# Feed-forward products by seven: two of the four weight sums per block as accumulating transfers, their products one step later, and an eighth raw weight tile

## The chip, the core and the metric

The kernel runs on one core of one Trainium2 chip. The metric is the device time of one execution in microseconds (us), as the median of several runs. TensorE (PE) multiplies, with its weight loads shown apart as PEld; VectorE is DVE, ScalarE is ACT, GpSimd is POOL, and SyncE is SP, which here only issues transfers. [...]

## What is computed

Two decoder layers on 256 tokens of width 2048, all in float32. Each layer has a mixing part (a gated spatial unit beside windowed attention) and a feed-forward part. The change touches the feed-forward part and, by the same function, the product for the attention queries.

```python
for l in range(DEPTH):                       # DEPTH = 2
    h = rms_norm(x, norm1_g[l])
    z = h @ w_in[l]                          # u, v, q, k, v columns
    ...                                      # spatial gating and attention
    x = x + mixed @ w_out[l]
    h2 = rms_norm(x, norm2_g[l])             # 256 x 2048
    x = x + (jax.nn.silu(h2 @ w_gate[l]) * (h2 @ w_up[l])) @ w_down[l]   # D_FF = 5632
```

## The kernel before, in words

**Products in three matmuls.** A float32 weight tile of 128x1024 (512 KB) is loaded into a tile called `raw` by SP (line 103, `raw_load`). `split2` splits it in two float32r parts: ACT casts it to `wh` (line 112), and DVE subtracts, `wl = raw - wh` (line 113). Each product of 128 columns is then three matmuls of 128x512 (lines 146 to 148): wh with the high part of the activations, wl with the high part, wh with the low part. There are seven raw tiles, five wh and four wl. A load on SP waits until a raw tile comes free, which is when the last DVE instruction that reads it is done; loads stand in one order on SP's queue.

**Units.** A standard unit (`unit`, line 150) is one raw tile and 12 matmuls into two PSUM banks (`dacc` or `acc`): the down projection, one gate-and-up block of the eleven, the input and output projections. A half unit (`s_unit` inside `seven`, line 300) is one raw tile and 6 matmuls into one bank `m0` to `m4`.

**Seven products instead of eight.** `seven` (line 297) treats gate and up (the two column halves) and even and odd rows of the weights as a 2x2 matrix, and computes it with seven half-size products. It has four steps, i = 0 to 3, and then eight half units. A step loads three raw tiles: `b11` (gate, even), `b12` (up, even) and `b22` (up, odd), and makes three sums of 128x1024:

- `b11 += b12` on DVE (line 328), for product m1;
- `t2 = b11 + b22` on DVE (line 329), for product m3;
- `b12 += b22` for product m2. On DVE it is line 335. In the query product of the first layer alone (`s_by_dma`) it is line 331 instead: POOL issues a transfer that reads b22's weights from memory again and adds them into b12.

After m3's split POOL issues a second accumulating transfer, which adds the fourth weight (gate, odd) into t2 (line 337); t2 is kept for the eight half units at the end. The half units of a step stand in the order m0, m1, m3, m4, m2 (in a call with `soon`, m4 comes second in its first step).

**The order of the work.** Ten of eleven gate-and-up blocks go through `seven` in each layer (20 blocks in all), 30 half units each. Between them standard units of the down projection are dealt out in a fixed share (83 units to 300 half units, about 1.4 per step). The program is written in this order; a scheduler then sets the order on each engine from the dependencies and its own costs, so the built order is what the excerpts below show. The query products are dealt out between the units of the input projection by the same means (`q_to`).

**Others on POOL's queue.** In the first layer POOL's queue also holds the power of the RMS norms (`ir`, line 202), the load of the gating weights `wm` (line 596, after the first `ir`) and an `AFFINE_SELECT` on them (line 597), which zeroes the upper triangle.

Of the kernel before, what the change touches and what calls it, by code (L numbers as in the profile page):

```python
# [12 lines left out]
F32 = mybir.dt.float32  # L13
# [7 lines left out]
P = 128  # L21
# [13 lines left out]
NB = 512  # L35
# [6 lines left out]
S_BLOCKS = (1, 2, 3, 4, 5, 6, 7, 8, 9, 10)  # L42
# [39 lines left out]
def trunk(ctx, tc, x, xt, w_in, w_q, w_out, w_gate, w_up, w_down, sgu_w, sgu_g, consts,  # L82
# [4 lines left out]
    wp = ctx.enter_context(tc.tile_pool(name="wp", bufs=1))  # L87
# [9 lines left out]
        return t.bitcast(F32)  # L97

    def raw_load(src, parts=1):
        raw = wp.tile([P, 2, NB], F32, tag="raw", name="raw", bufs=7)  # L100
        n = 2 // parts
        for i in range(parts):
            nc.sync.dma_start(raw[:, i * n : (i + 1) * n, :], src[:, i * n : (i + 1) * n, :])
        return raw

    def split2(raw):
        wh = wp.tile([P, 2, NB], F32R, tag="wh", name="wh", bufs=5)
        wl = wp.tile([P, 2, NB], F32R, tag="wl", name="wl", bufs=4)
        step = 2 if clock[0] > 1 else 1
        for j in range(0, 2, step):  # L110
            src = raw[:, j : j + step, :]
            nc.scalar.copy(wh[:, j : j + step, :], src)  # L112
            nc.vector.tensor_tensor(  # L113
                wl[:, j : j + step, :], src, f(wh[:, j : j + step, :]), ALU.subtract
            )
        return wh, wl
# [5 lines left out]
    def later(delay, fn):  # L122
        pending.append((clock[0] + delay, next(serial), fn))

    def tick(w=1.0):
        clock[0] += w
        due = sorted((e for e in pending if e[0] <= clock[0]), key=lambda e: e[:2])
        pending[:] = [e for e in pending if e[0] > clock[0]]
        for e in due:
            e[2]()  # L130
# [14 lines left out]
    def mm3(acc, ah, al, wh, wl, first, last, again=False):  # L145
        nc.tensor.matmul(acc, ah, wh, start=first, stop=False, skip_group_check=again)  # L146
        nc.tensor.matmul(acc, ah, wl, start=False, stop=False, skip_group_check=again)  # L147
        nc.tensor.matmul(acc, al, wh, start=False, stop=last, skip_group_check=again)  # L148

    def unit(src, acts, acc, first, last, again=False):  # L150
        raw = raw_load(src, 2 if clock[0] < 4 else 1)
        wh, wl = split2(raw)
        for j in range(2):
            act, aj = acts[j]
            for t in range(NTOK):
                ts = slice(t * P, (t + 1) * P)
                mm3(
                    acc[t], act[:, 0, aj, ts], act[:, 1, aj, ts], wh[:, j, :], wl[:, j, :],
                    first and j == 0, last and j == 1, again,
                )  # L160
        tick()
# [132 lines left out]
        extend(g, ap, "big", ext)  # L294
        return pair

    def seven(src, pairs, ext, out, end=lambda sg: None, soon=False, s_by_dma=False):
        bank = [pa.tile([P, NB], F32, tag="acc", name=f"m{i}") for i in range(5)]

        def s_unit(raw, m, i, op, first, last):  # L300
            wh, wl = split2(raw)
            for j in range(2):
                ah, al = (op(2 * i + j, h) for h in range(2))
                mm3(
                    bank[m], ah, al, wh[:, j, :], wl[:, j, :], first and j == 0,
                    last and j == 1, m in (0, 2),
                )
            tick(0.5)

        def a_op(k, t):  # L310
            return lambda p, h: pairs[p][:, h, k, t * P : (t + 1) * P]

        def e_op(n):
            return lambda p, h: ext[p][:, h, n, :]

        kept = []
        for i in range(4):
            b11 = raw_load(src(0, 0, i))
            b12 = raw_load(src(0, 1, i))
            b22 = raw_load(src(1, 1, i))  # L320
            t2 = ap.tile([P, 2, NB], F32, tag="spt", name="t2", bufs=4)
            first, last = i == 0, i == 3
            s_unit(b11, 0, i, a_op(0, 0), first, last)
            yield
            if soon and first:
                s_unit(b22, 4, i, e_op(3), first, last)
                yield
            nc.vector.tensor_tensor(b11, b11, b12, ALU.add)  # L328
            nc.vector.tensor_tensor(t2, b11, b22, ALU.add)
            if s_by_dma:  # L330
                nc.gpsimd.dma_start(b12, src(1, 1, i), accum_op=ALU.add)
            s_unit(b11, 1, i, e_op(1), first, last)
            yield
            if not s_by_dma:
                nc.vector.tensor_tensor(b12, b12, b22, ALU.add)
            s_unit(t2, 3, i, e_op(2), first, last)
            nc.gpsimd.dma_start(t2, src(1, 0, i), accum_op=ALU.add)  # L337
            yield
            if not (soon and first):
                s_unit(b22, 4, i, e_op(3), first, last)  # L340
                yield
            s_unit(b12, 2, i, e_op(0), first, last)
            yield
            kept.append(t2)
        m0, c12, c21, c22 = (
            zp.tile([P, NB], F32, tag="z", name=v) for v in ("m0", "c12", "c21", "c22")
        )
        nc.scalar.copy(m0, bank[0])
        nc.vector.tensor_tensor(m0, bank[3], m0, ALU.add)
        yield  # L350

        def add(out, x, y):
            nc.vector.tensor_tensor(out, x, y, ALU.add)

        steps = {
            0: lambda: add(c21, bank[2], m0),
            1: lambda: (nc.scalar.copy(bank[2], c21), add(c12, bank[1], m0)),
            2: lambda: (add(c22, bank[1], c21), add(c12, bank[4], c12)),
            5: lambda: out(0, bank[0], m0, c12),
        }  # L360
        for i in range(8):
            if i < 4:
                s_unit(raw_load(src(1, 0, i)), 0, i, a_op(1, 0), False, i == 3)
            else:
                s_unit(kept[i - 4], 2, i - 4, a_op(1, 1), False, i == 7)
            yield
            steps.get(i, lambda: None)()
        later(1, lambda: out(1, bank[2], c21, c22))
        end([m0, c21])
        yield  # L370

    def q_product(lay, pairs, ext):
        q = {"k": 0}
        q["steps"] = seven(
            lambda r, c, i: w_q[lay, c, i, r], pairs, ext, lambda *a: q["out"](*a),
            soon=True, s_by_dma=lay == 0,
        )
        return q

# [29 lines left out]
    for i in range(2 * NTOK):  # L409
        later(7 + 2.5 * i, lambda i=i: load_x(i // 2, i % 2))  # L410
    now_q = q_product(0, pairs1, ext1)

    for lay in range(L):
# [370 lines left out]
        def release(live=live, held=held, act_T=act_T):  # L784
            while held and live[0] < ACT_TILES:
                live[0] += 1
                act_T(*held.pop(0))

        def act_later(b, sg, held=held, release=release):
            for c in range(2):  # L790
                def ready(c=c):
                    held.append((b, c, sg))
                    release()

                later(2 + c, ready)
# [5 lines left out]
        def s_block(b, lay=lay, pairs2=pairs2, ext2=ext2, gated=gated, act_later=act_later):  # L801
            return seven(
                lambda r, c, i: (w_gate, w_up)[c][lay, b, i, r], pairs2, ext2, gated,
                lambda sg: act_later(b, sg), soon=b == S_BLOCKS[0],
            )

        seven_done = [False]
# [1 line left out]
        def s_stream(s_block=s_block):  # L809
            for b in S_BLOCKS:  # L810
                yield from s_block(b)
# [123 lines left out]
        if lay < L - 1:  # L935
            now_q = q_product(lay + 1, pairs1, ext1)
# [97 lines left out]
```

## Time and profile before

| | us |
|---|---|
| median of 3 runs | 1926.99 (1926.62 to 1929.71) |
| the profiled execution's own time | 1928.89 |
| its span in the trace | 1927.1 |
| PE busy | 1914.2 (99%), clock 1.0 |
| DVE busy | 1734.8 (90%) |
| ACT busy | 1341.1 (70%) |
| POOL busy | 150.5 (8%) |
| transfers, mean rate | 225 GB/s, 432.71 MB |

The busy share of PE says only that some matmul was in flight: a matmul of 128x512 takes about 390 ns and the next one starts 227 ns later, so PE can lose some 160 ns at a start before an idle stretch shows. What PE waits for is therefore read from PEld, whose loads carry the waits. The feed-forward parts run from about 300 to 930 us and from about 1256 to 1890 us of the span; in them the row of tenths for DVE stands at 9 throughout.

### The profile page before, as it was taken

What the parts mean: (1) busy time and instruction counts of PE and PEld (TensorE: products, weight loads), DVE (VectorE), ACT (ScalarE), POOL (GpSimd) and SP (SyncE); (2) the same over time, 40 slices, a digit from 0 to 9 for tenths busy, and PEclk for the clock granted to TensorE, in tenths of its full rate; (3) what the DMA queues carried; (4) which work ended last, traced back from release to release, by engine and by line L of the source; (5) the groups of instructions that cost most, each with busy time, mean ns of one, the idle gap of its engine ahead of it and who ended that gap; (6) DMA issues with size and microseconds to landing.
All of it is one profiled execution on the core that took longest, in us unless ns stands there. A gap on an engine that the chain in (4) does not pass through costs nothing.

```text
span 1927.1 us, 25136 instructions
## 1 busy us (share of the span) xinstructions
PE 1914.2 (99%) x8788; PEld 1568.1 (81%) x8788; DVE 1734.8 (90%) x1866; ACT 1341.1 (70%) x1799; POOL 150.5 (8%) x132
## 2 busy tenths in 40 slices
PE   9999999999999999999999999999999999999999
PEld 7788888877888888888888888888878888888887
DVE  7986689999999999999896767799999999999993
ACT  8768577677677676777777576666777677666674
POOL 0511000000000000000011200000000000000000
PEclk9999999999999999999999999999999999999999
DMA  9964347768777787778567534576778777867773
GB/s 337 283 255 155 136 159 219 239 217 274 210 239 242 248 258 222 224 237 277 190 216 260 184 128 165 176 244 208 236 246 257 225 225 245 274 207 242 240 260 122
DMA packets 120943, 432.71 MB, mean 225 GB/s; under 512 B 13424, under 2 KB 14064, under 8 KB 120816
## 3 DMA queue, kind: packets, MB, share of 16 engines
q1 hardware_dynamic: 105264, 375.52, 52.9%
q0 software_dynamic: 14976, 54.53, 15.5%
q8 instruction: 69, 1.13, 0.2%
q10 hardware_dynamic: 576, 1.05, 0.2%
q14 instruction: 58, 0.48, 0.1%
HBM read 428.95 MB, written 2.10 MB: 224 GB/s over the span
## 4 chain that ended last, share of the span: by engine, by line
PE 91%; DVE 3%; ACT 2%; issue 2%; DMA 1%; SPq 0%; POOL 0%; ACTq 0%; DVEq 0%; POOLq 0%
PE m L147 13%; PE m L148 13%; PE m L146 13%; PE dacc L146 10%; PE dacc L147 10%; PE dacc L148 10%; PE acc L146 6%; PE acc L147 5%; PE acc L148 5%; DVE wl L113 2%; ACT wh L112 1%; PE ps_v L568 1%; PE ps_f L219 1%; DMA raw<-in_w_in_dram 1%; PE ps_s L519 1%
## 5 line engine op out<-in xcount | busy, mean ns | idle before, releaser
L112 ACT CAST wh<-raw 128x1024 fp32r<-128x1024 f32 (+1 forms) x794 | 812.5, 1049 | 413.6 <-DVE raw L328 202.7
L113 DVE TENSOR_TENSOR wl<-raw,wh 128x1024 fp32r<-128x1024 f32 (+1 forms) x794 | 945.9, 1219 | 85.0 <-PE acc L147 28.5
L146 PE MATMUL m<-wh,ext 128*128 128x512 f32 x704 | 277.3, 395 | 1.6 <-ACT wh L112 1.6
L147 PE MATMUL m<-wl,ext 128*128 128x512 f32 x704 | 277.5, 394 | 1.4 <-DVE wl L113 1.4
L148 PE MATMUL m<-wh,ext 128*128 128x512 f32 x704 | 274.8, 390 | 0.0
L147 PE MATMUL dacc<-wl,aT 128*128 128x512 f32 x624 | 243.7, 391 | 0.3
L146 PE MATMUL dacc<-wh,aT 128*128 128x512 f32 x624 | 242.1, 392 | 1.8 <-ACT wh L112 1.8
L148 PE MATMUL dacc<-wh,aT 128*128 128x512 f32 x624 | 243.2, 390 | 0.0
L113 DVE TENSOR_TENSOR wl<-t,wh 128x1024 fp32r<-128x1024 f32 x176 | 212.3, 1220 | 5.6 <-PE dacc L147 3.0
L112 ACT CAST wh<-t 128x1024 fp32r<-128x1024 f32 x176 | 184.3, 1051 | 31.6 <-PE m L148 11.7
L146 PE MATMUL m<-wh,hT 128*128 128x512 f32 x528 | 205.6, 389 | 0.0
L148 PE MATMUL m<-wh,hT 128*128 128x512 f32 x528 | 205.4, 389 | 0.0
L147 PE MATMUL m<-wl,hT 128*128 128x512 f32 x528 | 205.4, 389 | 0.0
L147 PEld LDWEIGHTS m<-wl,ext 128*128 128x128 f32 x704 | 132.2, 188 | 36.2 <-DVE wl L113 9.3
L337 POOL DMA_DIRECT2D t<-in_w_gate_dram x80 | 69.7, 871 | 1149.7 <-DVE wl L113 1096.5
L146 PEld LDWEIGHTS m<-wh,ext 128*128 128x128 f32 x704 | 132.0, 188 | 30.9 <-ACT wh L112 4.5
L148 PEld LDWEIGHTS m<-wh,ext 128*128 128x128 f32 x704 | 132.2, 188 | 26.0
L146 PEld LDWEIGHTS dacc<-wh,aT 128*128 128x128 f32 x624 | 116.8, 188 | 28.5 <-ACT wh L112 4.0
L147 PEld LDWEIGHTS dacc<-wl,aT 128*128 128x128 f32 x624 | 117.2, 188 | 26.1 <-DVE wl L113 1.5
L148 PEld LDWEIGHTS dacc<-wh,aT 128*128 128x128 f32 x624 | 117.1, 188 | 24.3
L146 PE MATMUL acc<-wh,aT 128*128 128x512 f32 x336 | 135.0, 402 | 0.0
L148 PE MATMUL acc<-wh,aT 128*128 128x512 f32 x336 | 131.5, 391 | 0.0
(150 smaller groups left out, 2807.9 us busy)
## 6 DMA issues: line engine op xcount, KB each, us to landing
raw<-in_w_gate_dram SPq DMA_DIRECT2D x176, 512.0 KB, 5.6
raw<-in_w_up_dram SPq DMA_DIRECT2D x176, 512.0 KB, 5.6
raw<-in_w_down_dram SPq DMA_DIRECT2D x176, 512.0 KB, 4.6
t<-in_w_gate_dram POOLq DMA_DIRECT2D x80, 512.0 KB, 5.9
raw<-in_w_in_dram SPq DMA_DIRECT2D x76, 512.0 KB, 5.1
raw<-in_w_out_dram SPq DMA_DIRECT2D x64, 512.0 KB, 3.3
raw<-in_w_q_dram SPq DMA_DIRECT2D x32, 512.0 KB, 5.0
t<-in_w_q_dram POOLq DMA_DIRECT2D x8, 512.0 KB, 7.0
```

Of the source, the lines that this page charges most:

```text
L112: nc.scalar.copy(wh[:, j : j + step, :], src)
L113: nc.vector.tensor_tensor(wl[:, j : j + step, :], src, f(wh[:, j : j + step, :]), ALU.subtract)
L146: nc.tensor.matmul(acc, ah, wh, start=first, stop=False, skip_group_check=again)
L147: nc.tensor.matmul(acc, ah, wl, start=False, stop=False, skip_group_check=again)
L148: nc.tensor.matmul(acc, al, wh, start=False, stop=last, skip_group_check=again)
L219: nc.tensor.transpose(ps[:, j, t * P : (t + 1) * P], blocks[t][:, j * P : (j + 1) * P], ident)
L337: nc.gpsimd.dma_start(t2, src(1, 0, i), accum_op=ALU.add)
L519: nc.tensor.matmul(ps[r][:, i, :], qT[gp][rows, i0 + i, t * P : (t + 1) * P], kT[rows, gp, :nk], start=True, stop=True,)
L568: nc.tensor.matmul(pv[:, r, i], pt[:, (r * n + i) * (t + 1) + b, :], zkv[b][:, cols], start=b == 0, stop=b == t,)
```

## The change

In every block of `seven` in the feed-forward part the sum `b12 += b22` of steps 0 and 2 is made by an accumulating transfer on POOL, as the first layer's query product did it before in all four steps. Steps 1 and 3 keep the sum on DVE. A product whose sum is made by transfer is put off, unless its step is the last: it is issued in the next step, after that step's m3 and before its m4. This holds for the query product of the first layer too, whose steps 0, 1 and 2 now put off their product. The raw tiles become eight.

```diff
-        raw = wp.tile([P, 2, NB], F32, tag="raw", name="raw", bufs=7)
+        raw = wp.tile([P, 2, NB], F32, tag="raw", name="raw", bufs=8)
...
-    def seven(src, pairs, ext, out, end=lambda sg: None, soon=False, s_by_dma=False):
+    def seven(src, pairs, ext, out, end=lambda sg: None, soon=False, by_dma=()):
...
         kept = []
+        before = []
         for i in range(4):
...
             nc.vector.tensor_tensor(b11, b11, b12, ALU.add)
             nc.vector.tensor_tensor(t2, b11, b22, ALU.add)
-            if s_by_dma:
+            if i in by_dma:
                 nc.gpsimd.dma_start(b12, src(1, 1, i), accum_op=ALU.add)
             s_unit(b11, 1, i, e_op(1), first, last)
             yield
-            if not s_by_dma:
+            if i not in by_dma:
                 nc.vector.tensor_tensor(b12, b12, b22, ALU.add)
             s_unit(t2, 3, i, e_op(2), first, last)
             nc.gpsimd.dma_start(t2, src(1, 0, i), accum_op=ALU.add)
             yield
+            if before:
+                s_unit(*before.pop())
+                yield
             if not (soon and first):
                 s_unit(b22, 4, i, e_op(3), first, last)
                 yield
+            kept.append(t2)
+            if i in by_dma and not last:
+                before.append((b12, 2, i, e_op(0), first, last))
+                continue
             s_unit(b12, 2, i, e_op(0), first, last)
             yield
-            kept.append(t2)
...
-            soon=True, s_by_dma=lay == 0,
+            soon=True, by_dma=range(4 if lay == 0 else 0),
...
-                lambda sg: act_later(b, sg), soon=b == S_BLOCKS[0],
+                lambda sg: act_later(b, sg), soon=b == S_BLOCKS[0], by_dma=(0, 2),
```

Lines from 297 on shift by one to eight in the changed kernel: the sums 328 and 329 become 329 and 330, the accumulation into b12 becomes 332, the sum on DVE 336, the accumulation into t2 338.

DVE, step 2 of a block in the first feed-forward part, as built before. raw_4618, raw_4620 and raw_4622 are b11, b12 and b22 of the step, t2_4624 its t2; raw_4647 belongs to a standard unit.

```order
L328 TENSOR_TENSOR raw_4618<-raw_4618,raw_4620 128x1024
L329 TENSOR_TENSOR t2_4624<-raw_4618,raw_4622 128x1024
L113 TENSOR_TENSOR wl_4638<-raw_4618,wh_4637 128x1024
L113 TENSOR_TENSOR wl_4650<-raw_4647,wh_4649 128x1024
L335 TENSOR_TENSOR raw_4620<-raw_4620,raw_4622 128x1024
L113 TENSOR_TENSOR wl_4667<-t2_4624,wh_4666 128x1024
L113 TENSOR_TENSOR wl_4678<-raw_4622,wh_4677 128x1024
L113 TENSOR_TENSOR wl_4688<-raw_4620,wh_4687 128x1024
```

The sum into b12 (L335) and the split of b12 (the last row) both stand inside the step.

The same place on DVE in the changed kernel, with the same tile numbers for the step.

```order
L329 TENSOR_TENSOR raw_4618<-raw_4618,raw_4620 128x1024
L330 TENSOR_TENSOR t2_4624<-raw_4618,raw_4622 128x1024
L113 TENSOR_TENSOR wl_4639<-raw_4618,wh_4638 128x1024
L113 TENSOR_TENSOR wl_4651<-raw_4648,wh_4650 128x1024
L113 TENSOR_TENSOR wl_4667<-t2_4624,wh_4666 128x1024
L113 TENSOR_TENSOR wl_4678<-raw_4622,wh_4677 128x1024
```

The sum into b12 is gone from the step, and so is its split. Five rows of 128x1024 of step 3 and of a standard unit follow on DVE (the split and the two sums of step 3's b11, raw_4687, among them), and then:

```order
L113 TENSOR_TENSOR wl_4725<-raw_4687,wh_4724 128x1024
L336 TENSOR_TENSOR raw_4689<-raw_4689,raw_4691 128x1024
L113 TENSOR_TENSOR wl_4736<-t2_4693,wh_4735 128x1024
L113 TENSOR_TENSOR wl_4747<-raw_4620,wh_4746 128x1024
L113 TENSOR_TENSOR wl_4757<-raw_4691,wh_4756 128x1024
```

The split of b12 of step 2 (wl_4747<-raw_4620) has moved to step 3, where the sum of step 3 still stands on DVE: 12 rows of 128x1024 now lie between the sum that releases the transfer (raw_4618<-raw_4618,raw_4620) and the split.

POOL, during the first layer's query product, as built before. raw_536 and raw_687 are b12 of steps 1 and 2, t2_540 and t2_691 their t2; ir2 is the power of the layer's norm, ir16 that of a gating norm.

```order
L202 TENSOR_TENSOR ir2_632<-ms2_630,mhalf_99 128x2
L596 DMA wm_723<-in_sgu_w_dram 128x1024
L331 DMA raw_536<-in_w_q_dram 128x1024
L597 AFFINE_SELECT wm_723<-wm_723 128x1024
L337 DMA t2_540<-in_w_q_dram 128x1024
L331 DMA raw_687<-in_w_q_dram 128x1024
L337 DMA t2_691<-in_w_q_dram 128x1024
L202 TENSOR_TENSOR ir16_775<-ms16_773,mhalf_99 128x16
```

And in the changed kernel, where raw_500 and raw_677 are b12 of steps 1 and 2:

```order
L332 DMA raw_500<-in_w_q_dram 128x1024
L338 DMA t2_504<-in_w_q_dram 128x1024
L202 TENSOR_TENSOR ir2_632<-ms2_630,mhalf_99 128x2
L603 DMA wm_726<-in_sgu_w_dram 128x1024
L604 AFFINE_SELECT wm_726<-wm_726 128x1024
L332 DMA raw_677<-in_w_q_dram 128x1024
L338 DMA t2_681<-in_w_q_dram 128x1024
L202 TENSOR_TENSOR ir16_776<-ms16_774,mhalf_99 128x16
```

Both transfers of step 1 have moved ahead of the norm's power and of the `AFFINE_SELECT`; both transfers of step 2 and ir16 now stand right behind the `AFFINE_SELECT`.

DVE at ir16's place, before; v is the tile that is scaled with ir16, raw_687 the b12 of step 2.

```order
L200 TENSOR_SCALAR ms16_773<-hs8_770 128x16
L113 TENSOR_TENSOR wl_789<-raw_689,wh_788 128x1024
L113 TENSOR_TENSOR wl_801<-raw_798,wh_800 128x1024
L113 TENSOR_TENSOR wl_817<-raw_687,wh_816 128x1024
L113 TENSOR_TENSOR wl_829<-raw_826,wh_828 128x1024
L113 TENSOR_TENSOR wl_852<-raw_844,wh_851 128x1024
L629 TENSOR_TENSOR v_743<-v_743,ir16_775 128x512
```

In the changed kernel:

```order
L200 TENSOR_SCALAR ms16_774<-hs8_771 128x16
L113 TENSOR_TENSOR wl_824<-raw_816,wh_823 128x1024
L113 TENSOR_TENSOR wl_836<-raw_833,wh_835 128x1024
L329 TENSOR_TENSOR raw_816<-raw_816,raw_818 128x1024
L636 TENSOR_TENSOR v_744<-v_744,ir16_776 128x512
```

Three rows instead of five stand between the input of ir16 (ms16) and the first instruction that needs its result.

## The prediction

> **What bounds the kernel now.** First the page's busy times, then a table by stretches for the two feed-forward parts.
>
> ```profile
> PE 1914.2 (99%) x8788; PEld 1568.1 (81%) x8788; DVE 1734.8 (90%) x1866; ACT 1341.1 (70%) x1799; POOL 150.5 (8%) x132
> ```
>
> ```profile
> core 0: us, PE busy (x) PEld busy (x) DVE busy (x) ACT busy (x) POOL busy (x), PEclk, DMA share, GB/s
> 300.00:930.00 630.00, 628.18 (x2794) 513.89 (x2794) 616.21 (x578) 443.48 (x514) 34.66 (x40) 1.00 0.74 240
> 1256.00:1890.00 634.00, 632.15 (x2812) 517.28 (x2811) 618.53 (x580) 446.76 (x518) 35.01 (x40) 1.00 0.74 239
> ```
>
> PE is busy all through, at full granted clock (1.00), but DVE is at 616.21 of 630 us, 98%: two engines are full at once. Which one sets the pace is seen in PE's rhythm. The timeline of an undisturbed moment:
>
> ```profile
> 603.46 0.39 PE L146 MATMUL m<-wh,hT 128*128 128x512 f32 x1
> 603.46 0.19 PEld L147 LDWEIGHTS m<-wl,hT 128*128 128x128 f32 x1
> 603.69 0.39 PE L147 MATMUL m<-wl,hT 128*128 128x512 f32 x1
> ```
>
> A matmul starts every 0.23 us (603.46, 603.69), its weight load of 0.19 us starts with the matmul before it, so a load can come some 0.04 us late without cost. Now a disturbed moment, PE alone:
>
> ```profile
> 395.75 0.39 PE L148 MATMUL m<-wh,hT 128*128 128x512 f32 x1
> 396.39 0.50 PE L146 MATMUL m<-wh,ext 128*128 128x512 f32 x1 [0.25 <-ACT wh L112]
> 397.33 0.50 PE L146 MATMUL dacc<-wh,aT 128*128 128x512 f32 x1 [0.44 <-ACT wh L112]
> ```
>
> The starts are 0.64 and 0.94 us apart instead of 0.23: PE lost over 1.1 us here, waiting for a cast. So PE sets the pace and DVE's fullness costs only such moments. How much they are in all is in the waits of the two stretches (us in total, times, longest), first 300 to 930:
>
> ```profile
> PEld m L147 <- DVE wl L113: 3.4, 15, 0.3
> PEld m L146 <- ACT wh L112: 2.2, 5, 0.9
> PEld dacc L146 <- ACT wh L112: 2.0, 3, 0.9
> ACT wh L112 <- DVE raw L328: 98.8, 34, 4.4
> ACT wh L112 <- DMA raw<-in_w_gate_dram: 1.2, 1, 1.2
> ```
>
> then 1256 to 1890:
>
> ```profile
> PEld m L147 <- DVE wl L113: 3.4, 15, 0.3
> PEld m L146 <- ACT wh L112: 2.3, 5, 1.0
> PEld dacc L146 <- ACT wh L112: 2.0, 3, 0.9
> ```
>
> PE's loads waited 7.6 us in 23 waits, and 7.7 us in 23. ACT's late casts are DVE's doing: ACT waited 98.8 us for the sum of line 328. Of each wait about 0.08 us is free (0.04 us is idle before a load anyway, 0.04 us can be late), 23 x 0.08 = 1.8 us. PE thus lost about 5.8 and 5.9 us: **11.7 us is all that a lighter DVE can win in the feed-forward part**, 0.6% of the time, whatever it saves on DVE.
>
> **The change part by part.** *The sums.* Removed are 20 blocks x 2 steps = 40 DVE instructions of line 335.
>
> ```profile
> L335 DVE TENSOR_TENSOR raw<-raw 128x1024 f32<-128x1024 f32 x84 | 102.4, 1219 | 0.0
> ```
>
> 40 x 1.219 = 48.8 us, 2.4 us per block of about 62 us, against a loss of 0.58 us per block (11.7 / 20). The built order agrees: 84 - 40 = 44 sums remain on DVE, and 40 transfers more stand on POOL. DVE's saving is four times the loss, but it falls in steps 0 and 2, and steps 1 and 3 keep three sums each, one after the other with the put-off split between them. I take three quarters of 11.7: **-8.8 us** (bounds 0 and -11.7).
>
> *The moved products.* A put-off product is one cast, one split and six matmuls, none added. PE's count stays. What can be late next is the b12 transfer. It is released by the sum of line 329 of the changed kernel, and b12's split follows 12 rows of 128x1024 later. The pitch of such rows, from two in a row of line 113:
>
> ```profile
> 599.72 2.36 DVE L113 TENSOR_TENSOR wl<-t,wh 128x1024 fp32r<-128x1024 f32 x2
> ```
>
> 2.36 - 1.22 = 1.14 us, so 12 x 1.14 = 13.7 us, less 1.3 us for the cast ahead of it: b12 must have landed 12.4 us after its release (11.2 us in the tightest blocks, where 11 rows lie between). What such transfers took, in us from issue, first line 331 and then line 337, one answer each:
>
> ```profile
> DMA to landing us min/median/max: 5.4/7.5/8.9
> ```
>
> ```profile
> DMA to landing us min/median/max: 5.2/5.9/9.3
> ```
>
> Even 9.3 us leaves 1.9 us. POOL's queue ahead of it holds only the last step's t2 transfer, which is older. Cost taken **0**; the far bound is a rival below. ACT takes its casts in order, so a late b12 would hold every cast behind it.
>
> [...]
>
> *The transfers.* Shares of the queues and the landing of plain loads, from the page:
>
> ```profile
> q1 hardware_dynamic: 105264, 375.52, 52.9%
> q0 software_dynamic: 14976, 54.53, 15.5%
> ...
> raw<-in_w_gate_dram SPq DMA_DIRECT2D x176, 512.0 KB, 5.6
> ...
> raw<-in_w_out_dram SPq DMA_DIRECT2D x64, 512.0 KB, 3.3
> ```
>
> q0 took 15.5% of 1927.1 us = 299 us for 54.53 MB, 2.9 us per 512 KB; q1 1.4 us. Forty more are 115 us in 1264, so the share of 0.74 becomes about 0.83. Loads in the part without accumulating transfers (w_out) land in 3.3 us, beside them (w_gate) in 5.6: a transfer on POOL costs a load near it 2.3 us. Against it stands the eighth tile. From the SP queue's own waits, 300 to 930:
>
> ```profile
> SPq L103 <- DVE wl L113: 534.9, 247, 6.6
> ```
>
> Practically every load waits for a tile to come free, one per 630 / 247 = 2.55 us, so one tile more starts a load 2.55 us earlier; while b12 is held longer, that tile is spent on it and the others have seven as before. Today 40 such transfers in this stretch cost one wait for a load, 1.2 us (row above). Twenty more in proportion cost 0.6 us, in both stretches **+1.2 us** (bounds -1, if the tile wins, and +10, half a microsecond for each of 20 blocks, about the present loss over again).
>
> *The query product of layer 0.* Its put-off products end one wait. Waits in the first 100 us:
>
> ```profile
> ACT wh L112 <- DMA raw<-in_w_q_dram: 3.2, 1, 3.2
> PEld m L147 <- DVE wl L113: 2.6, 4, 1.5
> ```
>
> Of these PE can win at most 2.6 us. But POOL's queue is rearranged. The rows around the `AFFINE_SELECT`, POOL and then DVE:
>
> ```profile
> 52.16 14.74 POOL L597 TENSOR_SCALAR_AFFINE_SELECT wm<-wm 128x1024 f32<-128x1024 f32 x1 [1.23 <-DMA wm<-in_sgu_w_dram]
> 66.85 0.88 POOL L337 DMA_DIRECT2D t<-in_w_q_dram  x1
> ```
>
> ```profile
> 64.72 1.22 DVE L328 TENSOR_TENSOR raw<-raw 128x1024 f32<-128x1024 f32 x1
> 65.97 2.00 DVE L329 TENSOR_TENSOR t<-raw 128x1024 f32<-128x1024 f32 x1
> ```
>
> ```profile
> L597 POOL TENSOR_SCALAR_AFFINE_SELECT wm<-wm x4: 1087/1109/14739, 52.2 to 1068.1; 128x1024 f32<-128x1024 f32 x4
> ```
>
> It took 14.74 us here, 1.1 us elsewhere, and ended when DVE first paused (65.94 to 65.97); the DVE row that met it took 2.00 us instead of 1.22. Back-to-back DVE rows hold POOL off. Behind it now stand both transfers of step 2 and ir16, with three DVE rows of cover (3.4 us) instead of five (5.7). If POOL is held again, DVE itself stops at the scaling by ir16, which lets POOL in: 1.1 for the select, 2 x 0.9 for the transfers and about 3 for ir16, some 6 us less 3.4 of cover: up to +3, and +6 if step 2's transfer is late too. I take **0** (bounds -2.6 and +6).
>
> [...]
>
> *Sum:* -8.8 + 0 + 1.2 + 0 = -7.6 us on the profiled execution's 1928.89 (span 1927.1 and 1.8 around it): 1921.3. That execution is 1.9 us above the median of the runs; on 1926.99 it is **1919.4**.
>
> **The rivals.** (1) *The whole loss goes*, and the query product's wait too: 1926.99 - 11.7 - 2.6 = 1912.7. For it: DVE's saving is four times the loss. Against: the sums left stand in bursts. (2) *The gain is eaten by loads*: the share of the transfers, already above 0.9 in parts of a block, rises where the two accumulations of a step meet.
>
> ```profile
> 640.00:650.00 10.00, 10.00 (x46) 8.10 (x45) 9.93 (x9) 6.37 (x8) 0.66 (x1) 1.00 0.91 293
> 650.00:660.00 10.00, 10.00 (x46) 8.29 (x45) 10.00 (x13) 9.22 (x13) 0.21 (x1) 1.00 0.94 312
> ```
>
> At +8 for loads: 1926.99 - 8.8 + 8 = 1926. Against: even at 0.94 PE stayed at 10.00 of 10. (3) *POOL is held in the first layer*: -7.6 + 5 gives 1924.4. For it the row of 14.74 us; against, the three other selects of that line took 1.1 us, DVE's pauses having let them in. (4) *The put-off products wait for their transfers, slower*: it decides at a landing of 11.2 to 12.4 us. With step and t2 transfers in the rings together, 9.3 + 2.9 = 12.2 us, about 1 us late in half of 40 places; ACT holds all casts, the gain is gone too: 1927 + 20 = 1947. Against: the two are released some 4 rows (4.6 us) apart. (5) *The change does nothing of what it says*: excluded by the built order.
>
> **How the numbers follow.** Forecast (own range 1914 to 1923) 0.55, rival (1) 0.07, (2) 0.12, (3) 0.10, (4) 0.16. A measurement of this kernel can tell about 0.2% (3.9 us) from no change: below 1923.1 is faster, above 1930.8 slower. Faster 0.62 (forecast and 1), same 0.22 (2 and 3), slower 0.16 (4). For 8 in 10 the range leaves out most of rival 4 and the lower half of rival 1: 1913 to 1932.
>
> **What would show it.** Right: in both feed-forward stretches DVE falls by 24 us, PEld's waits for wl and wh fall from 7.6 to below 3 us, the line of b12's accumulation has no row in ACT's waits, and loads of gate land in about 6 us. Wrong: ACT waiting for a transfer into raw from w_up in many places (rival 4), ACT or DVE waiting for plain loads (2), DVE waiting for ir in the first 100 us (3). A span that falls by more than 14 us would mean that PE's rhythm itself was slowed by something that I did not see.

## The result, and the profile after

The changed kernel takes **1922.45 us** (median of 8 runs, 1921.59 to 1923.66). The kernel before, run again beside it, takes 1927.53 us (8 runs). The ratio is 0.9974, 95% interval [0.9963, 0.9984]: 5.1 us less (interval 3.1 to 7.1). The forecast was 1919.4, which is 7.6 us less. The profiled execution took 1923.14 us, with a span of 1921.4.

The page of the changed kernel: busy times, the queue q0, and the landing of the transfers.

```profile
PE 1911.6 (99%) x8788; PEld 1571.9 (82%) x8788; DVE 1695.4 (88%) x1826; ACT 1343.7 (70%) x1799; POOL 174.6 (9%) x172
...
q0 software_dynamic: 20736, 75.51, 21.2%
...
raw<-in_w_gate_dram SPq DMA_DIRECT2D x176, 512.0 KB, 6.1
...
raw<-in_w_up_dram POOLq DMA_DIRECT2D x40, 512.0 KB, 5.9
```

DVE has 40 instructions fewer (1866 to 1826), POOL the 40 new transfers into b12, which land in 5.9 us. They are what q0 carries more: 75.51 MB instead of 54.53, which is 40 x 512 KB. Plain loads of gate land in 6.1 us instead of 5.6, about the 6 that was expected.

The two feed-forward stretches of the changed kernel, with the columns as in the prediction:

```profile
300.00:930.00 630.00, 630.00 (x2812) 518.64 (x2811) 600.40 (x563) 447.48 (x517) 51.01 (x59) 1.00 0.83 257
...
1256.00:1890.00 634.00, 634.00 (x2830) 521.98 (x2829) 600.12 (x561) 451.04 (x522) 51.59 (x59) 1.00 0.83 257
```

How much faster a stretch became can be read from the count behind PE's time. A stretch has a fixed length here, so a faster kernel fits more matmuls in: 2812 against 2794, and 2830 against 2812. At a pitch of 0.227 us, 18 more matmuls are 4.1 us, in both stretches together **8.2 us**. DVE fell by 15.8 and 18.4 us and not by the 24 us that the prediction named as a sign. The removed rows are gone in full (40 sums of line 335 became 20 of line 336 in each stretch, 24.4 us); the 18 matmuls brought two splits of their own into the same stretch, 2.4 us, and the rest of the difference was not followed up. The DMA share rose from 0.74 to 0.83, as worked out.

The waits from 300 to 930 in the changed kernel:

```profile
PEld m L147 <- DVE wl L113: 0.8, 3, 0.4
PEld m L146 <- ACT wh L112: 0.5, 2, 0.3
PEld dacc L146 <- ACT wh L112: 0.4, 1, 0.4
```

The three rows that held 7.6 us hold 1.7 us. So the feed-forward part did what was forecast, and a little more. Yet the whole kernel gained 5.1 us. Some 3 us were given back elsewhere, and the stretch from 50 to 100 us shows where: before, and then in the changed kernel.

```profile
50.00:100.00 50.00, 47.67 (x211) 38.58 (x211) 47.48 (x58) 33.76 (x41) 28.10 (x10) 1.00 0.95 286
```

```profile
50.00:100.00 50.00, 47.40 (x201) 37.97 (x200) 44.00 (x56) 33.03 (x42) 17.53 (x11) 0.97 0.90 277
```

Ten matmuls fewer in the query product of the first layer (2.3 us), a granted clock of 0.97 instead of 1.00, and DVE 3.5 us *less* busy. The count of before is that of one execution; in the profiles of the experiments below that keep its query product it is 214 to 218. An engine that was full now waits. The waits of the first 100 us in the changed kernel name for what:

```profile
ACT zkv L466 <- POOL ir L202: 3.7, 1, 3.7
...
DVE ext L284 <- ACT ext L283: 2.5, 1, 2.5
```

The timeline there, POOL, then ACT, then DVE, then PE (start, duration, engine; in brackets how long the engine had waited, and for what):

```profile
57.30 3.29 POOL L202 TENSOR_TENSOR ir<-ms,mhalf 128x2 f32<-128x2 f32 x1 [3.81 <-DVE ms L200]
```

```profile
60.63 0.72 ACT L466 ACTIVATE zkv<-zkv,ir 128x512 f32<-128x512 f32 x1 [3.74 <-POOL ir L202]
```

```profile
58.80 1.21 DVE L113 TENSOR_TENSOR wl<-raw,wh 128x1024 fp32r<-128x1024 f32 x1
62.51 0.69 DVE L284 TENSOR_TENSOR ext<-e,ext 128x512 fp32r<-128x512 f32 x1 [2.49 <-ACT ext L283]
```

```profile
65.74 0.50 PE L146 MATMUL m<-wh,ext 128*128 128x512 f32 x1 [1.50 <-ACT wh L112]
67.06 0.56 PE L147 MATMUL m<-wl,ext 128*128 128x512 f32 x1 [0.81 <-DVE wl L113]
67.42 0.63 PE L148 MATMUL m<-wh,ext 128*128 128x512 f32 x1
67.84 0.63 PE L146 MATMUL m<-wh,ext 128*128 128x512 f32 x1
```

Read from the top: the power of the norm, 256 numbers on POOL, took 3.29 us, and in the kernel before 0.71:

```profile
46.20 0.71 POOL L202 TENSOR_TENSOR ir<-ms,mhalf 128x2 f32<-128x2 f32 x1 [2.90 <-DVE ms L200]
```

There DVE's next row needed `ir` itself, so DVE stood still beside it:

```profile
46.94 0.22 DVE L426 TENSOR_SCALAR nr<-ir 128x1 f32<-128x1 f32 x2 [0.83 <-POOL ir L202]
```

In the changed kernel other rows follow behind `ms`, and DVE ran on. `ir` ended at 60.59, 0.58 us after DVE's row of 58.80 had run out (60.01). ACT waited for it with the cast of `ext` queued behind, DVE for that cast; so DVE's sums came late, and PE stopped twice. After that its matmuls started 0.42 us apart (67.42, 67.84) instead of 0.23.

The theory to be tested has two parts. **FF**: a lighter DVE gives some 8 us in the feed-forward part, the transfers cost little, and putting off is what hides them. **Query**: the 3 us are lost in the first layer because back-to-back DVE rows with two SBUF operands keep POOL's `ir` waiting. Rivals: the eighth tile gives the gain and the sums do nothing; the loads pay for the transfers; the query product merely stands in a worse order, and `ir` fills a wait that is there anyway.

### The profile page after: what moved, and what is told of

It reads as the page before. It is cut to its first block, busy times and chain, and to the rows that moved or that the text cites. A ratio compares the mean times of both kernels' runs of the same rounds, so it can differ in the third digit from the quotient of the medians.

```text
span 1921.4 us, 25385 instructions
## 1 busy us (share of the span) xinstructions
PE 1911.6 (99%) x8788; PEld 1571.9 (82%) x8788; DVE 1695.4 (88%) x1826; ACT 1343.7 (70%) x1799; POOL 174.6 (9%) x172
## 3 DMA queue, kind: packets, MB, share of 16 engines
q0 software_dynamic: 20736, 75.51, 21.2%
q8 instruction: 69, 1.13, 0.2%
## 4 chain that ended last, share of the span: by engine, by line
PE 94%; DVE 2%; ACT 1%; issue 1%; DMA 1%; POOL 1%; SPq 0%; ACTq 0%; DVEq 0%; POOLq 0%
PE m L147 14%; PE m L146 14%; PE m L148 14%; PE dacc L146 10%; PE dacc L147 10%; PE dacc L148 10%; PE acc L146 5%; PE acc L148 5%; PE acc L147 5%; PE ps_f L219 1%; PE ps_v L575 1%; DVE wl L113 1%; DMA raw<-in_w_in_dram 1%; POOL ir L202 1%; PE ps_s L526 1%
## 5 line engine op out<-in xcount | busy, mean ns | idle before, releaser
L112 ACT CAST wh<-t 128x1024 fp32r<-128x1024 f32 x176 | 184.3, 1051 | 37.3 <-DVE t L330 13.7
L147 PE MATMUL acc<-wl,aT 128*128 128x512 f32 x336 | 130.9, 390 | 0.0
```

## The experiments

Ratios are against the kernel before, run beside each.

**The feed-forward part alone.** The change without putting off in the query product, whose program is then as before:

```diff
-            if i in by_dma and not last:
+            if off and i in by_dma and not last:
...
-            soon=True, by_dma=range(4 if lay == 0 else 0),
+            soon=True, by_dma=range(4 if lay == 0 else 0), off=False,
```

> The change in the feed-forward part alone: the first layer's query product takes its sums by transfer but puts no product off, as the kernel before did; the eighth tile stays. The theory (the feed-forward part won about 8.4 us, of which the rearranged query product gave back 3) expects 1919 us, 8 to 9 us below the kernel before, and no ACT wait for ir in the first 100 us. The rival (it is the eighth tile or the fuller queues that slow the first 100 us, not the put-off products) expects 1922 to 1923, as the changed kernel.

Measured: 1919.85 us (1919.31 to 1921.34), 0.9961 [0.9948, 0.9973]. Its rows from 50 to 100, 300 to 930 and 1256 to 1890:

```profile
50.00:100.00 50.00, 48.68 (x217) 39.69 (x216) 49.18 (x62) 34.47 (x42) 23.03 (x10) 1.00 1.00 299
...
300.00:930.00 630.00, 629.83 (x2811) 518.30 (x2810) 597.93 (x559) 447.47 (x521) 51.11 (x59) 1.00 0.83 256
...
1256.00:1890.00 634.00, 634.00 (x2831) 522.08 (x2830) 599.72 (x560) 450.91 (x522) 50.80 (x58) 1.00 0.82 255
```

The feed-forward part keeps its gain, and the query product loses nothing: `ir` takes 0.71 us again, with DVE standing still beside it. The `AFFINE_SELECT` behind it was held here too, for 9.64 us, but nobody waited for it. This version beats both kernels: 7.7 us below before, 2.6 below the change.

**The eighth tile alone**, the kernel before with eight raw tiles:

```diff
-        raw = wp.tile([P, 2, NB], F32, tag="raw", name="raw", bufs=7)
+        raw = wp.tile([P, 2, NB], F32, tag="raw", name="raw", bufs=8)
```

> The kernel before with eight raw tiles instead of seven and nothing else. The theory (the sums taken from VectorE win the time, the tile only pays for the longer hold of b12) expects 1926 to 1928 us, within 1 us of the kernel before, with DVE still at 616 us busy of 630 and PE's loads still waiting 7 us in each feed-forward part. The rival (loads that start one tile earlier are what wins) expects 1920 to 1922.

Measured: 1927.73 us (1927.21 to 1928.44), 1.0001 [0.9992, 1.001]. Without the change the tile is worth nothing; the rival that it gives the gain falls.

**The change without it**, seven raw tiles:

```diff
-        raw = wp.tile([P, 2, NB], F32, tag="raw", name="raw", bufs=8)
+        raw = wp.tile([P, 2, NB], F32, tag="raw", name="raw", bufs=7)
```

> The whole change with seven raw tiles instead of eight. The theory (b12 is held some 12 us longer in two steps of four and so takes a tile from the loads; the eighth gives it back) expects 2 to 5 us more than the changed kernel, 1925 to 1927, with ACT or DVE waiting for plain loads. The rival (the loads have slack enough) expects 1922 to 1923, as with eight.

Measured: 1936.18 us (1932.61 to 1937.02), 1.0038 [1.0026, 1.0051]: 13.7 us above the change. The expectation was far off. Waits from 300 to 930:

```profile
DVE wl L113 <- ACT wh L112: 17.0, 18, 3.2
...
ACT wh L112 <- DMA raw<-in_w_down_dram: 9.6, 4, 4.6
```

and PE's weight loads in the same stretch:

```profile
PEld m L147 <- DVE wl L113: 6.5, 12, 1.0
```

ACT now waits for *plain* loads, which start too late. The kernels differ in the number of tiles alone, so it is a tile that the loads lack: a put-off b12 keeps its own for most of another step. Nothing waited for the accumulating transfer itself. The tile is worth nothing alone and 13.7 us inside the change: it pays for the putting off.

**Transfers, but nothing put off** in either place; eight tiles:

```diff
-            if i in by_dma and not last:
+            if off and i in by_dma and not last:
...
-                lambda sg: act_later(b, sg), soon=b == S_BLOCKS[0], by_dma=(0, 2),
+                lambda sg: act_later(b, sg), soon=b == S_BLOCKS[0], by_dma=(0, 2), off=False,
```

> The sums of steps 0 and 2 by transfer as in the change, but every product in its own step, and the query product as before. In its own step the split of b12 follows five or six rows of 128x1024 after the sum that releases the transfer, 6 to 7 us, less 1.3 us for the cast, where a transfer takes 5 to 9 us to land. The theory (putting off is what hides the transfer) expects ACT to wait 1 to 3 us at most of the 40 places and 1930 to 1960 us. The rival (the split's lead over TensorE absorbs it) expects 1919 to 1923.

Measured: 1962.72 us (1959.41 to 1967.92), 1.0184 [1.0167, 1.0202], a little above the expected range. Waits and stretch from 300 to 930:

```profile
ACT wh L112 <- DMA raw<-in_w_up_dram: 27.8, 11, 4.7
```

```profile
300.00:930.00 630.00, 617.52 (x2727) 501.75 (x2726) 585.85 (x549) 432.32 (x502) 51.02 (x59) 1.00 0.81 251
```

84 matmuls fewer than with putting off (2811): 19 us in one stretch. Over the whole run ACT waited for the transfers of line 332 for 64.6 us, in 26 waits; in the changed kernel nobody did. Putting off hides the landing of the transfer, and is worth about 43 us against the first experiment. Some of this is PE's clock, whose mean in the four executions was 0.995 to 0.999.

**The lighter DVE alone**: the kernel before, which leaves out the sum `b12 += b22` of steps 0 and 2 (product m2 then uses b12 as loaded):

```diff
-            if not s_by_dma:
+            if not s_by_dma and i not in left_out:
...
-                lambda sg: act_later(b, sg), soon=b == S_BLOCKS[0],
+                lambda sg: act_later(b, sg), soon=b == S_BLOCKS[0], left_out=(0, 2),
```

> The kernel before, seven tiles, with the DVE sum into b12 left out in steps 0 and 2 of the 20 feed-forward blocks and nothing put in its place, so that m2 is computed from b12 without b22 there. It shows what a lighter VectorE alone is worth, with no transfer, no moved product and no tile. The theory expects 1917 to 1919 us, 8.5 to 10 us below the kernel before, PE's loads waiting under 2 us in each feed-forward part. The rival (the gain needs the order in which products are put off) expects less than 4 us, 1923 to 1927.

Measured: 1918.32 us (1917.9 to 1920.7), 0.9955 [0.9941, 0.9968]: **9.2 us** less than before, with the order of the products untouched. So the gain does not need the products to be put off, and the rival falls.

**The transfers alone**: the kernel before, which keeps all its sums and adds up's odd weights into t2 by a third transfer in steps 0 and 2 (so t2 holds one weight too many):

```diff
             nc.gpsimd.dma_start(t2, src(1, 0, i), accum_op=ALU.add)
+            if i in more:
+                nc.gpsimd.dma_start(t2, src(1, 1, i), accum_op=ALU.add)
...
-                lambda sg: act_later(b, sg), soon=b == S_BLOCKS[0],
+                lambda sg: act_later(b, sg), soon=b == S_BLOCKS[0], more=(0, 2),
```

> The kernel before with 40 accumulating transfers added and nothing removed: in steps 0 and 2 of the feed-forward blocks up's odd weights are added into t2 behind the first accumulation, so t2 holds one weight too many. It shows what the transfers themselves cost. The theory (about 1 us in all, the loads have cover) expects 1927 to 1930 us. The rival (the 2.3 us later landing of loads reaches TensorE with only seven tiles) expects 1933 to 1940 and ACT waiting for plain loads.

Measured: 1928.75 us (1927.12 to 1930.0), 1.0005 [0.9996, 1.0013]. Forty more transfers of 512 KB cost about **1.2 us**, which the interval (-0.8 to +2.5 us) does not tell from nothing. The two parts measured by themselves, -9.2 and +1.2, make -8.0; the first experiment, which has both, the tile and the putting off, gave -7.7.

**Three steps instead of two**, query product as before, eight tiles:

```diff
-                lambda sg: act_later(b, sg), soon=b == S_BLOCKS[0], by_dma=(0, 2),
+                lambda sg: act_later(b, sg), soon=b == S_BLOCKS[0], by_dma=(0, 1, 2),
```

> The query product as before, and in the feed-forward blocks the sums of steps 0, 1 and 2 by transfer, all three products put off, eight tiles: 20 sums fewer on VectorE and 20 transfers more than the change has. The theory (what the change left of TensorE's waits is about 1.5 us in each feed-forward part, and the transfers then fill 0.87 of the time) expects 1917 to 1919 us, at most 2 us below the change with the query product as before. The rival (loads and put-off products now wait for the rings, with two tiles held at a time) expects 1922 to 1935.

Measured: 1925.27 us (1923.34 to 1932.31), 0.999 [0.9981, 0.9999]: 5.4 us worse than two steps, and inside the rival's range. Its stretch and waits from 300 to 930:

```profile
300.00:930.00 630.00, 628.05 (x2803) 516.92 (x2802) 587.27 (x548) 444.64 (x516) 59.69 (x69) 1.00 0.86 264
```

```profile
ACT wh L112 <- DMA raw<-in_w_down_dram: 17.3, 6, 4.5
```

DVE is another 13 us lighter than in the change, but the plain loads are late again, as with seven tiles, and that costs more. The rival names two reasons, fuller queues and two tiles held at a time. The accumulating transfers land later too, in 7.1 us (median) instead of 5.9, plain loads of gate in 5.9 instead of 6.1; the run does not separate the two. Whether a ninth tile would mend it was not tried.

**The query product: `ir` earlier.** The changed kernel with the first layer's norm begun 2.5 units sooner:

```diff
-        later(1 if lay > 0 else 18, begin)
+        later(1 if lay > 0 else 15.5, begin)
```

> The changed kernel with one number altered: the first layer's norm is begun at 15.5 units instead of 18, so that its sum and ir2 stand some six rows earlier on VectorE and ahead of ScalarE's need. The theory (ScalarE waits 3.7 us for ir2, which comes late and is held off on POOL by VectorE, and TensorE stops for it twice) expects 2.5 to 3.5 us less than the changed kernel, about 1919 us, and no ACT wait for ir before 70 us. The rival (TensorE stops there for the sums over late loads or for the transfers of the query product) expects no change, 1922 to 1923.

Measured: 1923.22 us (1922.56 to 1924.38), 0.9978 [0.9969, 0.9987]: no gain, against the expectation. POOL:

```profile
52.85 7.34 POOL L202 TENSOR_TENSOR ir<-ms,mhalf 128x2 f32<-128x2 f32 x1
```

and DVE's last row before its pause:

```profile
58.40 1.21 DVE L113 TENSOR_TENSOR wl<-raw,wh 128x1024 fp32r<-128x1024 f32 x1
```

`ir` began 4.45 us sooner and ended at 60.19 instead of 60.59, again 0.58 us after DVE's unbroken run of rows (59.61). An earlier start does not help here; `ir` ended only when DVE paused. And DVE paused there only because ACT stood behind `ir`: the wait had to be made before it could end.

**A pause made for it.** If it takes two operands from SBUF to hold POOL off, which no run had shown so far, a DVE instruction that reads one should leave POOL its way. The changed kernel with a sum that is used by nobody, three rows behind `ms`:

```diff
+        if gap:
+            void = small([P, n], "void2")
+            nc.vector.tensor_reduce(void, bc(ms, 512), AX.X, ALU.add)
```

> The changed kernel with one more VectorE instruction in the first layer's norm: a sum over 128x(2x512) broadcast elements, about 1.2 us, which reads one operand from SBUF and not two, placed three rows behind ms so that it runs beside POOL's ir. Its result is not used. Theory (POOL's ir is held as long as VectorE's two-operand rows follow one another without a gap): ir takes about 1 us instead of 3.3 to 7.3 us, ScalarE's wait of 3.7 us for it goes, the stop of TensorE at 64 to 67 us and its 8 matmuls at half rate behind it go, and the time falls by 2 to 3 us below that of the changed kernel, to 1919.5 to 1920.5 us, although VectorE has 1.2 us more to do. Rival (the order of the put-off products or late loads stops TensorE there, and ir only fills the wait): 1922 to 1924 us, with ir short and TensorE still stopped by about 2 us near 65 us.

Measured: 1921.73 us (1921.1 to 1922.65), 0.9964 [0.995, 0.9978], the kernel before being at 1928.89 beside it. Neither expectation was met. POOL and DVE:

```profile
57.30 1.82 POOL L205 TENSOR_TENSOR ir<-ms,mhalf 128x2 f32<-128x2 f32 x1 [3.81 <-DVE ms L200]
```

```profile
58.46 1.21 DVE L204 TENSOR_REDUCE void<-ms 128x2 f32<-128x1024 f32 x1
61.03 0.69 DVE L287 TENSOR_TENSOR ext<-e,ext 128x512 fp32r<-128x512 f32 x1 [1.36 <-ACT ext L286]
```

`ir` ended 0.66 us after the new row had begun (58.46 to 59.12), in the middle of it and with DVE busy. But DVE's wait of 2.49 us became one of 1.36 plus 1.21 us for the new row: the pause had been bought from the engine that was short of time. The size I expected forgot that price.

**The pause sooner and shorter, and its control.** The same sum with half the length directly behind `ms`, and in a second kernel, at the same place, an addition with two operands from SBUF:

```diff
+        if gap:
+            with tc.issue_after(m.ins):
+                void = small([P, n], "void2")
+                nc.vector.tensor_reduce(void, bc(mhalf[:, :n], 256), AX.X, ALU.add)
```

```diff
-                void = small([P, n], "void2")
-                nc.vector.tensor_reduce(void, bc(mhalf[:, :n], 256), AX.X, ALU.add)
+                void = zp.tile([P, n, 256], F32, tag="z", name="void2")
+                half = bc(mhalf[:, :n], 256)
+                nc.vector.tensor_tensor(void, half, half, ALU.add)
```

> The changed kernel with one more VectorE instruction in the first layer's norm, now directly behind ms and half as long: a sum over 128x(2x256) broadcast elements, about 0.6 us, with one operand from SBUF; its result is not used. Theory (POOL's ir is held only while VectorE's two-operand rows follow one another): ir is done within 1 us of its start, ScalarE's wait for it falls from 3.7 us to about 1 us, VectorE's wait of 2.5 us for ext goes, its sum of raw in the query product ends some 1.5 us sooner, TensorE's stop at 64 to 67 us goes for the most part, and the time is 1919.5 to 1920.5 us against the changed kernel's 1922.45. Rival (TensorE is stopped there by the order of the query product's rows whatever ir does): 1921.5 to 1923 us.

> The same kernel with the same place for the added VectorE instruction, but with two operands from SBUF: an addition over 128x512 elements, about 0.7 us; its result is not used. Theory (the port): ir is not done beside it and ends in VectorE's first pause, 3 us or more behind its start; the time is 1922 to 1924 us. Rival (any instruction at this place, or the new order around it, brings the gain): ir within 1 us and the time of the run with one operand.

Measured: one operand 1920.24 us (1919.28 to 1920.93), 0.996 [0.9948, 0.9973]; two operands 1921.8 us (1921.31 to 1923.36), 0.9971 [0.9961, 0.9982]. The first met its expectation; the second stays just below what the theory expected, 1922 us and 3 us for `ir`. DVE and then POOL with one operand:

```profile
56.85 0.68 DVE L204 TENSOR_REDUCE void<-mhalf 128x2 f32<-128x512 f32 x1
```

```profile
57.03 0.71 POOL L206 TENSOR_TENSOR ir<-ms,mhalf 128x2 f32<-128x2 f32 x1 [3.81 <-DVE ms L200]
```

and with two:

```profile
56.88 0.68 DVE L205 TENSOR_TENSOR void<-mhalf 128x512 f32<-128x512 f32 x1
...
58.81 0.41 DVE L276 TENSOR_TENSOR e<-g 128x256 f32<-128x256 f32 x1
```

```profile
57.05 2.75 POOL L207 TENSOR_TENSOR ir<-ms,mhalf 128x2 f32<-128x2 f32 x1 [3.81 <-DVE ms L200]
```

The same place, the same 0.68 us of DVE, the same start of `ir`: 0.71 us beside one operand, 2.75 us beside two, where it ended 0.58 us after DVE's run of rows (59.22 to 59.80), for the third time. So it is what DVE runs beside `ir` that holds it, not the place or the order. The two added rows differ in one thing more: the sum writes 2 numbers per partition, the addition 512. That it is the reading and not the writing is not shown by this pair; it was my assumption. Nor does a run show what in the chip holds `ir`: the word port in the last expectation is only the theory's name for it. The hold lasted over whole runs of rows, 7.34 us at the longest, in the kernel with the norm earlier.

The hold can be followed down to PE. With one operand ACT waited 1.2 us for `ir`, DVE 0.46 us for `ext`; with two it was 3.2 and 1.88 us. PE with one operand, and then with two:

```profile
64.23 0.49 PE L146 MATMUL m<-wh,ext 128*128 128x512 f32 x1 [0.27 <-ACT wh L112]
65.18 0.73 PE L146 MATMUL dacc<-wh,hT 128*128 128x512 f32 x2 [0.45 <-ACT wh L112]
```

```profile
65.67 0.50 PE L146 MATMUL m<-wh,ext 128*128 128x512 f32 x1 [1.06 <-ACT wh L112]
66.62 0.73 PE L146 MATMUL dacc<-wh,hT 128*128 128x512 f32 x2 [0.44 <-ACT wh L112]
```

The rows from 60 to 70 with one operand and with two, and then of the changed kernel, two rows:

```profile
60.00:70.00 10.00, 9.24 (x39) 6.80 (x38) 10.00 (x13) 7.15 (x9) 3.75 (x3) 1.00 0.76 267
```

```profile
60.00:70.00 10.00, 8.15 (x32) 5.58 (x31) 8.90 (x13) 7.74 (x10) 3.61 (x2) 1.00 0.65 238
```

```profile
60.00:70.00 10.00, 7.68 (x28) 5.67 (x27) 7.51 (x10) 7.20 (x10) 3.20 (x4) 0.87 0.68 242
70.00:80.00 10.00, 10.00 (x44) 8.26 (x43) 8.02 (x11) 5.56 (x9) 3.72 (x2) 0.96 0.95 246
```

In these two executions with a row added PE's clock stayed full; in the changed kernel's it lacked 1.3 and 0.4 us of two slices of 10 us, 1.7 us in all. These are single executions. The mean granted clock of every execution, in thousandths, was 0.999 in 7 of 8 of the changed kernel, 1.000 in 5 of 5 of the first experiment, 1.000 in 4 of 5 with one operand, and 0.999 in 4 of 8 with two. The kernel before has 0.999 too, in 5 of the 21 executions beside the first experiment.

In time the hold is the larger part. The kernel with two operands is 1.56 us slower than the one with one, and no execution of the one reaches into the range of the other; 2.6 us were to be explained. Among executions at 1.000 alone the difference is 1.1 us (medians 1920.33 and 1921.46, four of each). The clock comes on top where it falls: with two operands the four executions at 0.999 have a median of 1922.70, 1.2 us more. In the changed kernel this cannot be seen: its one execution at 1.000 took 1923.18 us, among its slowest. How the rest of the 2.6 us divides is not settled.

## Why the prediction was right, point by point

**What bounds the kernel: right.** PE set the pace, DVE's fullness cost only moments. The limit of 11.7 us for a lighter DVE holds: leaving the sums out gained 9.2 us, and making them by transfer 7.7 in the version without the query product's change.

**The sums, -8.8: right**, by 9.2 measured alone. That three quarters of the loss would go was a choice; the runs give 9.2 / 11.7, 79%. The reason that went with it, that the sums left in steps 1 and 3 stand in bursts, is not shown: the run that relieved a third step, and should have told, met late loads.

**The moved products, 0: right as far as the waits show; it was not measured alone.** Nobody waited for line 332 in the changed kernel. It landed, in us from issue, in

```profile
DMA to landing us min/median/max: 5.0/5.9/8.9
```

against the 11.2 that were to spare. So rival 4 did not come. Its mechanism is real: without putting off, ACT waits 64.6 us for those transfers, and the kernel takes 1962.7 us. Only the point from which it decides was not reached. What the first experiment leaves for the moved products and the tile together is 0.3 us (-7.7 against the -8.0 of the two parts).

**The transfers, +1.2: right** by the transfers alone, 1.0005 [0.9996, 1.0013], that is +1.2 us. That the figure came out to the tenth is luck: the interval runs from -0.8 to +2.5. Rival 2 was wrong for two steps. But the sentence beside this number, "while b12 is held longer, that tile is spent on it and the others have seven as before", is right and was given no price: without the eighth tile the change loses 13.7 us, where I expected 2 to 5. Rival 2's sign, ACT waiting for plain loads, stood one tile away, and it is what happens in the third step.

**The query product, 0 (bounds -2.6 and +6): the step that failed.** It measured +2.6 (1922.45 against 1919.85), inside the bounds; it accounts for the difference between forecast and result, and the result lies between the forecast of 1919.4 and rival 3's 1924.4. I had rival 3's mechanism in hand, POOL held off by DVE's rows, but at the wrong instruction: I followed the `AFFINE_SELECT` and ir16 behind it, and expected DVE to wait at the scaling by ir16. The select was not held in the changed kernel:

```profile
66.78 1.18 POOL L604 TENSOR_SCALAR_AFFINE_SELECT wm<-wm 128x1024 f32<-128x1024 f32 x1 [5.60 <-DMA wm<-in_sgu_w_dram]
```

The one held was ir2 ahead of it, moved to a place beside a full DVE, and ACT waited for it with a cast behind that DVE needed. I had named the waits of every instruction behind the select, and not those of the one before. And of the three short selects of the kernel before only two met a pause of DVE (at 103.92 and 1032.19, 1.13 and 1.09 us); the third (1068.15, 1.09 us) began beside a `TENSOR_REDUCE` of 1067.10 to 1068.37 us. That PE's clock could fall after its stops (0.87 and 0.96 in two slices of 10 us) was not foreseen.

**The sum.** Forecast -8.8 + 0 + 1.2 + 0 = -7.6; measured -9.2, 0 (from the waits), +1.2 and +2.6, together -5.4, where the whole showed -5.1.

## What to carry to other kernels

Work that is moved off a full engine is worth what the other engine waits for it, not what it takes: 48.8 us of DVE were 9.2 us of time, and in a third step the late loads cost 5.4 us more than the lighter DVE gave. Whoever puts a product off to hide a transfer pays with the buffer that it keeps, 13.7 us here where it was missing; look for that buffer before looking at the transfer. And when a change moves instructions past one another, ask of each small one on POOL that an engine waits for what DVE does beside it: here a DVE row of 0.68 us with one SBUF operand, put directly behind what POOL waited for, took `ir` from 3.29 to 0.71 us and the time from 1922.45 to 1920.24 us. A held instruction that nobody waits for, as the `AFFINE_SELECT` of 9.64 us in the first experiment, needs none.

## What the runs showed of the hardware

**POOL was held for a run of DVE rows, not for one.** In the first layer's norm a power over 128x2 took 0.71 us beside a standing DVE (the kernel before) and beside a row with one SBUF operand put directly behind `ms`, and 1.82, 2.75, 3.29 or 7.34 us in the four other kernels shown. In the last three of these it ended 0.58 us after DVE's run of rows; in the one of 1.82 us it ended 0.66 us after a row with one SBUF operand had begun.

**After short stops PE's granted clock fell for some 3.4 us, but not each time.** In the changed kernel PE waited 1.50 and 0.81 us with one matmul in between; then its matmuls started 0.42 us apart instead of 0.23, from 67.42 to 70.81 us. The granted clock lacked 1.7 us in 20, half of these 3.4 us. In the profiled execution of the kernel with the late pause the slices lack 0.10 and 0.07, 1.7 us once more; in that of the kernel with the norm earlier 0.21 and 0.13, which is 3.4 us, an estimated 6.8 us at half rate:

```profile
60.00:70.00 10.00, 7.97 (x29) 5.65 (x28) 8.97 (x14) 6.36 (x9) 3.03 (x1) 0.90 0.64 245
70.00:80.00 10.00, 10.00 (x43) 8.21 (x42) 8.92 (x9) 6.93 (x10) 5.39 (x4) 0.93 0.92 228
```

```profile
60.00:70.00 10.00, 7.46 (x24) 4.95 (x24) 7.90 (x11) 7.29 (x9) 2.81 (x4) 0.79 0.60 196
70.00:80.00 10.00, 10.00 (x40) 8.09 (x40) 7.54 (x9) 5.97 (x9) 1.04 (x2) 0.87 1.01 291
```

The stops alone do not decide it. In the kernel with seven tiles the same two stops, 1.49 and 0.81 us with one matmul in between, left the next matmuls 0.23 us apart, at full clock:

```profile
65.56 0.51 PE L146 MATMUL m<-wh,ext 128*128 128x512 f32 x1 [1.49 <-ACT wh L112]
66.88 0.50 PE L147 MATMUL m<-wl,ext 128*128 128x512 f32 x1 [0.81 <-DVE wl L113]
67.21 0.39 PE L148 MATMUL m<-wh,ext 128*128 128x512 f32 x1
67.44 0.40 PE L146 MATMUL m<-wh,ext 128*128 128x512 f32 x1
```

What decides it is not shown. No stop of the changed kernel here was longer than 1.5 us, and PE worked in between; the like stops of these two kernels ended differently, and the kernel with two operands had a mean clock of 0.999 in four of its executions and of 1.000 in the four others.
